# Where the sums of the second MLP leave PSUM, and when GLA's share of the weight sums is made

## The chip, the core and the metric

The kernel runs on one core of a Trainium2 chip. Its engines work side by side, each through its own queue in order: TensorE (matmuls; PE in the profile, its weight loads PEld), VectorE (DVE), ScalarE (ACT), GpSimd (POOL), and SyncE (SP), which here only issues DMAs. A matmul writes its sums into one of eight PSUM banks, and VectorE or ScalarE has to carry them from there to SBUF before the bank can take the next sums. The metric is the device time of one execution in microseconds (us).

## The reference

Two layers over 272 tokens (16 meta tokens and 256 of the sequence) of width 2048. Layer 0 mixes tokens by RWKV-7, layer 1 by gated linear attention (GLA); behind each stands an MLP with squared ReLU:

```python
def sq_relu_mlp(x, w1, w2):
    h = jax.nn.relu(x @ w1)          # 2048 -> 8192
    return (h * h) @ w2              # 8192 -> 2048
...
h = h + mix_out
h = h + sq_relu_mlp(rms_norm(h, norm_mlp[i]), mlp_w1[i], mlp_w2[i])
...
return rms_norm(h, norm_f)[:, N_META:]
```

GLA projects its input to q (4 heads of 256), k (the same), v (4 heads of 512) and a gate (4 heads of 512), runs a chunked recurrence and projects back. Everything is float32; the meta tokens are dropped at the end, so the second MLP works on 256 tokens only.

## The kernel before

**Precision.** A float32 weight tile `raw` (128x1024) is split into two reduced-precision tiles: ScalarE casts it to `hi`, VectorE takes `lo = raw - hi`. The same is done to the moving operand. A float32 product is then three matmuls: hi by hi, hi by lo, lo by hi. So each weight tile costs a DMA, a cast on ScalarE and a subtraction on VectorE. That pair of cast and subtraction is called a split here.

**Order of the work.** RWKV, the first MLP (`mlp`, L268), GLA (`gla`, L1462) and the second MLP (`mlp1`, L371) follow each other. In RWKV partly, and in `mlp1` on all of TensorE, VectorE, ScalarE and SyncE, the order on each engine is that of the program text. In GLA a scheduler orders the queues.

**The second MLP.** The hidden width 8192 is taken in four blocks b of 2048. For each block, a *row* (L408) is a tile of 128 hidden features: two slots of eight wide (512 columns) and eight narrow (256) matmuls; then its two halves are joined (ScalarE copies one, VectorE adds the other), relu and square run on ScalarE, and the result is split into `hi` and `lo` of `HS`. The second matrix product is done in 2x2 blocks by Strassen's scheme in Winograd's form, with seven products for eight. A *unit* (b, g, p), L475, covers 256 hidden features p of block b and one half g of the output columns; the output stands as four quadrants `C[t, f]` in `htok`. A fast unit has four slots, A, B, E and G, with 2, 2, 2 and 1 products of three wide matmuls each. Its seven sums stay in seven PSUM banks `own[1]` to `own[7]` over all p of a phase. An ordinary unit (p beyond `FAST[b]`, block 3 only, where p = 0 to 3 are fast) has two slots with four plain products each, and no gain from the scheme.

The phases run in the order of `PHASES` (L53): (0,1) (0,0) (1,0) (1,1) (2,1) (2,0) (3,0) (3,1). Sums go on over two phases with the same g. So banks are emptied at the ends of phases 0, 2 and 4 (all units fast, `alone` in the code), and of phases 6 and 7 (block 3). In between, rows of this or the next block stand between the units, except before a phase's last unit or two. The four quadrants come out of the seven sums with `t1 = own[1]`, `u2 = own[6] + t1`, `u3 = own[7] + u2`, `u4 = own[5] + u2`:

| quadrant | is increased by, each times a scale per token `rs2` |
|---|---|
| `C[1,0]` | `t1`, `own[2]` |
| `C[1,1]` | `u4`, `own[3]` |
| `C[0,0]` | `u3`, `own[4]` |
| `C[0,1]` | `u3`, `own[5]` |

`into` (L486) is one such increase: one VectorE instruction over 128x512 which reads PSUM or SBUF, multiplies by `rs2` and adds `C`. `t1` and `u2` to `u4` lie in `hres`, the residual stream, which is dead by then; so does `nf`, the final norm's gains, loaded by DMA (L669) at slot 20.

**The stream of slots.** `stream` is the list of all slots. In step i the program emits first what was put down for before slot i, then the split of slot i + 3, then what was put down for behind it, then slot i's matmuls:

```python
for f in before.pop(i, []): f()
while done < min(len(stream), i + AHEAD + 1):   # AHEAD = 3
    split(done); done += 1
for f in behind.pop(i, []): f()
if i < len(stream): stream[i][1](sets.pop(i), i)
```

`later(slot, f, after)` (L391) puts f down for before a slot, or behind its splits where the third argument is true. There are five `raw` buffers and four pairs of `hi` and `lo`. A raw buffer is loaded anew when its split is done; A's and B's only when VectorE has formed, from both, the operand of slot G ("fourth", L641 ff.), a 128x512 subtraction.

**The last phase.** Its p run in the order 0, 4, 1, 5, 2, 3, 6, 7: fast units and ordinary ones in turn. The units p = 6 and 7 (`closes`) first do the products of banks 2 and 3 of all their slots, then those of the other two banks. `gain(t)` multiplies the finished half of `htok` by `nf` (VectorE, 128x1024); `empty` is the last `into` of a bank with the sum of squares on ScalarE; `norm` scales the rows and stores them.

**The weight sums.** The fast units' weights need differences of blocks of `mlp_w2`. These are made ahead: a step fetches three tiles (GpSimd's DMA queue), VectorE forms three differences (L351 to L353, each 128x512), and GpSimd stores them to `diff` in device memory. Of the 56 units, 44 are made in the first MLP and 12 in GLA, with two sets of three tiles in GLA. A unit is fetched in one step, formed in the next, stored in the one after, and so there are 14 steps in GLA. `ticks` (L319) spreads them: each call of `tick` counts up, and the step numbers up to calls x 14 // rows are then made, where `rows` is 27 (L1492). GLA calls `tick` after every key projection, value projection and gate projection, 2 + 4 + 4 times per head. A head's projections run q, k, q, k, four v, four gate; after the second and third gate projection, the next head's forget gates are made (`gate`, L1496, whose matmul L1498 goes to the one bank `pm` and whose VectorE reader is `mn`, L1505).

Of the kernel before, what the change touches and what calls it, by code (L numbers as in the profile page):

```python
# [19 lines left out]
D = 2048  # L20
KT = D // P
# [8 lines left out]
C = 64  # L30
# [30 lines left out]
class Kern:  # L61
# [309 lines left out]
    def mlp1(self, x, acc):  # L371
# [6 lines left out]
        htok = self.t(hp, [P, 2, D], "htok")  # L378
        flat = hres.rearrange("p k t -> p (k t)")
        nf = flat[:, :D]  # L380
        t1, u2, u3, u4 = (flat[:, D + 512 * i : D + 512 * i + 512] for i in range(4))
        ssq = self.t(hp, [P, 2, 4], "ssq")
        sum3 = self.t(hp, [P, 2], "sum3")
        rs2 = self.t(hp, [P, 2], "rs2")
# [6 lines left out]
        def later(slot, f, after=False):  # L391
            (behind if after else before).setdefault(slot, []).append(f)
# [82 lines left out]
        def unit(b, g, p):  # L475
# [20 lines left out]
            if p < FAST[b]:  # L496

                def pe(todo):
                    def run(w, slot):
                        H = hid[p]  # L500
                        for at, i, ws in todo:
                            product(at, (H[:, 0, i], H[:, 1, i]), w, ws, first, final_fast and (alone or at in (1, 5, 6, 7)))
                            if not final_fast:
                                continue
                            if at == 1:
                                later(slot + 1, lambda: nc.scalar.copy(t1, own[1]), True)
                            if at == 2 and alone:
                                later(slot + 1, lambda: into(1, 0, own[2]))
                            if at == 7:
                                later(slot + 1, lambda: (add(u2, own[6], t1), add(u3, own[7], u2)))  # L510
                            if at == 5:
                                later(slot + 2, lambda: (add(u4, own[5], u2), into(0, 1, own[5])))
                                if alone:
                                    later(slot + 3, lambda: into(1, 1, own[3]))
                                later(slot + 3, lambda: into(1, 0, t1))
                                later(slot + 4, lambda: into(1, 1, u4))
                                later(slot + 5, lambda: into(0, 0, u3))
                                later(slot + (5 if end else 6), lambda: into(0, 1, u3))
                            if at == 4 and alone:
                                later(slot + 2, lambda: into(0, 0, own[4]))  # L520
                    return run

                d = self.diff[b, g, p]
                todo = {"A": [(1, 0, one), (2, 2, two)], "B": [(6, 4, two), (7, 5, one)], "E": [(5, 3, two), (3, 6, one)],
                        "G": [(4, 1, one)]}
                srcs = {"A": [(both, w[:, :2])], "B": [(both, d[:, 1:])], "E": [(one, w[:, 2]), (two, d[:, 0])], "G": None}
                return [(srcs[k], pe(todo[k]), k) for k in "ABEG"]
# [14 lines left out]
            def pe(k):  # L542
                def run(w, slot):
                    H = hid[p]
                    if not closes:
                        for at in (2, 3, 4, spare):
                            ordinary(at, H, k, w, last and k == 1)
                        if last and k == 1:
                            for n, at in enumerate((2, 3, 4, spare)):
                                later(slot + 1 + n // 2, lambda at=at: empty(at))  # L550
                            if b == NHB - 1:
                                for n in range(4):
                                    later(slot + 4 + n, lambda n=n: final(n // 2, n % 2))
                        return
                    closing.append((H, k, w))
                    if p == KT // 2 - 2:
                        later(slot + 2, lambda: gain(1 - k))
                    for at in (2, 3):
                        ordinary(at, H, k, w, last and k == 1)
                    if last and k == 1:  # L560
                        empty(2)
                        empty(3)
                        most(1)
                        norm(1)
                        for at in (spare, 4):
                            for n, (X, m, pair) in enumerate(closing):
                                h, ws = places[at][2:]
                                product(at, (X[:, 0, 2 * m + h], X[:, 1, 2 * m + h]), pair, ws, False, n == 3)
                            empty(at)
                            if at == spare:  # L570
                                most(0)
                        norm(0)
                return run
# [3 lines left out]
        def gain(t):  # L577
            tt(htok[:, t, :1024], htok[:, t, :1024], nf[:, :1024], ALU.mult)
# [22 lines left out]
            row(0, f, (0, 4)[f % 2], f if f < 8 else None)  # L601
        for n, (b, g) in enumerate(PHASES):
            second, more = n % 2 == 1, b < NHB - 1
            for p in range(KT // 2) if more or not second else (0, 4, 1, 5, 2, 3, 6, 7):
                if second and more:
                    row(b + 1, p)
                elif not second and b and p < 7:
                    row(b, 9 + p)
                steps = unit(b, g, p)
                stream.extend(steps[:2])  # L610
                if second and more and p == 7:
                    row(b + 1, 8)
                stream.extend(steps[2:])
                if not b and not second and p < 6:
                    row(b, 10 + p)
# [38 lines left out]
        with tc.manual_schedule(engines=engines):  # L654
            load()
            done = 0
            for i in range(len(stream) + 8):
                for f in before.pop(i, []):
                    f()
                while done < min(len(stream), i + AHEAD + 1):  # L660
                    split(done)
                    done += 1
                for f in behind.pop(i, []):
                    f()
                if i < len(stream):
                    stream[i][1](sets.pop(i), i)
                if i == 10:
                    scales()
                if i == 20:  # L669
                    nc.sync.dma_start(nf, ap["nf"].to_broadcast([P, D]))  # L670
        es.close()

# [789 lines left out]
    def gla(self, x, rstd, hres, done):  # L1462
# [26 lines left out]
        pq = self.proj(pair(0), x, SEQ, NMETA)  # L1489
        rs = rstd[:, NMETA:]  # L1490
        left, oT = [[self.t(self.x2p, [P, 2, T], "x", KT) for _ in range(3)] for _ in range(2)], []
        tick = self.ticks(self.differences(slice(EARLY, None), lambda u: left[u % 2], 1), 27)  # L1492
        c0, c1, c2, c3 = (NMETA + C * i for i in range(4))
        gates = {}

# [25 lines left out]
        for hd in range(GH):  # L1521
# [105 lines left out]
            for v in range(4):  # L1627
# [5 lines left out]
                    finish(0, waiting, hr)  # L1633
                gt = self.t(gp, [P, SEQ], "gt", 2)
                tt(self.two(gt), pg, self.two(rs))
                tick(gt[:, :2])
                sg = self.t(gp, [P, SEQ], "sg", 2)
                nc.scalar.activation(sg, gt, AF.Abs)
                nc.scalar.activation(sg, sg, AF.Exp, scale=-1.0)
# [150 lines left out]
```

## Time and profile before

| | |
|---|---|
| median of 3 runs | 2362.39 us (2361.3 to 2363.02) |
| the profiled execution's own time | 2364.6 us |
| its span in the profile | 2362.5 us |
| second MLP within it | first row matmul at 1695.7 us, to the end |
| GLA within it | first forget gate at 1317 us, ends before the second MLP |

All durations below come from the one profiled execution. A line of a queue shows the start in us from the span's start, the duration, the engine, the line, the operation with output and input tiles, and in brackets how long the engine stood idle before it and which instruction's end let it go. In a list of waits stand the total in us, how often, and the longest. Matmuls overlap in their pipeline, so a matmul's bar is longer than its pitch. Tiles are named without numbers: `pu`, `pt`, `pm`, `pry` and `pj` are PSUM banks, which `mlp1` uses as `own[1]`, `own[2]` (`pu`), `own[7]`, `own[6]` (`pt`), `own[5]` (`pm`), `own[3]` (`pry`), `own[4]` and `own[0]` (`pj`).

### The profile page before, as it was taken

How to read it: one execution, taken by the hardware profiler on the slowest of the kernel's cores; microseconds unless marked ns; L12 is line 12 of the kernel's file. 1: busy time of each engine (PE TensorE's matmuls, PEld its weight loads, DVE VectorE, ACT ScalarE, POOL GpSimd, SP SyncE). 2: the span in 40 equal slices, each digit the busy share in tenths (PEclk: the TensorE clock that was granted, in tenths of full speed). 3: DMA queues.
4: the chain of work that ended last, by engine and by line, in shares of the span. 5: the costliest groups of instructions: out<-in, count | busy, mean ns of one | idle time of the engine just before them, and what ended most of it. 6: DMA issues, size and time to landing. Idle time of an engine off the chain costs nothing.

```text
span 2362.5 us, 48857 instructions
## 1 busy us (share of the span) xinstructions
PE 2318.0 (98%) x19183; PEld 2177.1 (92%) x19183; DVE 1821.3 (77%) x2976; ACT 1367.9 (58%) x2152; POOL 222.8 (9%) x541
## 2 busy tenths in 40 slices
PE   9999999999999999999999999999999999999997
PEld 8888888889999999999999999999998898998886
DVE  8868976848667667666666788877779889888877
ACT  6488645556555345345444555556576776776765
POOL 0000000000122222222220023100000000000000
PEclk9999999999999999999999999999999999999999
DMA  6459754535788888888885688755667777877875
GB/s 210 160 195 311 242 164 139 148 98 175 260 300 300 295 308 308 300 303 310 302 286 185 227 272 279 237 170 196 214 214 258 259 267 252 272 257 246 264 251 177
DMA packets 200326, 567.75 MB, mean 240 GB/s; under 512 B 41184, under 2 KB 56800, under 8 KB 199968
## 3 DMA queue, kind: packets, MB, share of 16 engines
q1 hardware_dynamic: 173216, 476.53, 59.6%
q0 software_dynamic: 26880, 88.10, 12.0%
q8 instruction: 151, 2.47, 0.4%
q14 instruction: 79, 0.65, 0.1%
HBM read 504.38 MB, written 58.46 MB: 238 GB/s over the span
## 4 chain that ended last, share of the span: by engine, by line
PE 82%; DVE 11%; ACT 3%; issue 2%; DMA 2%; SPq 0%; DVEq 0%; POOL 0%; ACTq 0%
PE pj L172 16%; PE pj L174 16%; PE pj L173 16%; PE pj L419 9%; PE pj L420 5%; PE pj L205 2%; DVE lo L150 2%; PE pj L206 1%; PE pu L492 1%; PE pu L494 1%; PE pu L493 1%; DVE lo L373 1%; DVE upd L676 1%; DVE sysA L676 1%; PE pt L494 1%
## 5 line engine op out<-in xcount | busy, mean ns | idle before, releaser
L149 ACT CAST hi<-raw 128x1024 fp32r<-128x1024 f32 (+1 forms) x562 | 526.2, 947 | 588.7 <-PE pj L173 508.8
L150 DVE TENSOR_TENSOR lo<-raw,hi 128x1024 fp32r<-128x1024 f32 (+1 forms) x562 | 613.0, 1100 | 247.9 <-ACT hi L149 243.1
L172 PE MATMUL pj<-x,hi 128*128 128x272 f32 (+1 forms) x2560 | 729.2, 285 | 2.0 <-DVE r L676 0.9
L174 PE MATMUL pj<-x,lo 128*128 128x272 f32 (+1 forms) x2560 | 715.3, 279 | 4.4 <-DVE lo L150 4.3
L173 PE MATMUL pj<-x,hi 128*128 128x272 f32 (+1 forms) x2560 | 714.2, 279 | 0.0
L172 PEld LDWEIGHTS pj<-x,hi 128*128 128x128 f32 x2560 | 485.5, 190 | 15.2 <-issue 7.1
L174 PEld LDWEIGHTS pj<-x,lo 128*128 128x128 f32 x2560 | 485.5, 190 | 6.9 <-DVE lo L150 6.6
L173 PEld LDWEIGHTS pj<-x,hi 128*128 128x128 f32 x2560 | 485.6, 190 | 2.5 <-issue 1.4
L373 DVE TENSOR_TENSOR lo<-raw,hi 128x1024 fp32r<-128x1024 f32 x368 | 411.2, 1140 | 72.6 <-ACT hi L641 67.7
L641 ACT CAST hi<-raw 128x1024 fp32r<-128x1024 f32 x368 | 351.5, 979 | 83.1 <-PE pj L419 26.3
L419 PE MATMUL pj<-x,hi 128*128 128x512 f32 x1024 | 341.8, 384 | 1.6 <-ACT hi L641 1.6
L172 PE MATMUL pj<-h,hi 128*128 128x272 f32 x1024 | 285.7, 279 | 0.0
L173 PE MATMUL pj<-h,hi 128*128 128x272 f32 x1024 | 285.7, 279 | 0.0
L174 PE MATMUL pj<-h,lo 128*128 128x272 f32 x1024 | 285.7, 279 | 0.0
L420 PE MATMUL pj<-x,lo 128*128 128x256 f32 x1024 | 280.7, 274 | 2.9 <-DVE lo L373 2.9
L419 PEld LDWEIGHTS pj<-x,hi 128*128 128x128 f32 x1024 | 194.3, 190 | 29.6 <-ACT hi L641 2.8
L420 PEld LDWEIGHTS pj<-x,lo 128*128 128x128 f32 x1024 | 197.2, 193 | 7.0 <-DVE lo L373 5.6
L172 PEld LDWEIGHTS pj<-h,hi 128*128 128x128 f32 x1024 | 193.5, 189 | 0.0
L173 PEld LDWEIGHTS pj<-h,hi 128*128 128x128 f32 x1024 | 193.5, 189 | 0.0
L174 PEld LDWEIGHTS pj<-h,lo 128*128 128x128 f32 x1024 | 193.5, 189 | 0.0
L359 POOL DMA_DIRECT2D diff<-x x168 | 91.6, 545 | 137.6 <-DVE x L353 52.5
L345 POOL DMA_DIRECT2D x<-w_d x168 | 90.1, 542 | 25.3 <-DMA diff<-x 22.8
(352 smaller groups left out, 3415.2 us busy)
## 6 DMA issues: line engine op xcount, KB each, us to landing
raw<-mlp_w_d SPq DMA_DIRECT2D x384, 512.0 KB, 4.9
raw<-gla_in_d SPq DMA_DIRECT2D x98, 512.0 KB, 4.3
x<-w_d POOLq DMA_DIRECT2D x168, 256.0 KB, 5.6
diff<-x POOLq DMA_DIRECT2D x168, 256.0 KB, 6.4
raw<-w_rkv_d SPq DMA_DIRECT2D x80, 512.0 KB, 3.8
raw<-w_d SPq DMA_DIRECT2D x72, 512.0 KB, 4.7
raw<-diff SPq DMA_DIRECT2D x56, 512.0 KB, 5.3
raw<-gla_o_d SPq DMA_DIRECT2D x32, 512.0 KB, 3.3
```

The costliest lines, as they stand in the source:

```text
L149: nc.scalar.copy(hi[:, h], raw[:, h])
L150: nc.vector.tensor_tensor(out=lo[:, h], in0=raw[:, h], in1=hi[:, h].bitcast(F32), op=ALU.subtract)
L172: nc.tensor.matmul(out, hi[:, ws], xh, start=first, stop=False)
L173: nc.tensor.matmul(out, hi[:, ws], xl, start=False, stop=False)
L174: nc.tensor.matmul(out, lo[:, ws], xh, start=False, stop=last)
L205: nc.tensor.matmul(wide, hi[:, ws], xt, start=kt == 0, stop=False)
L345: nc.gpsimd.dma_start(x[:, body], w[:, k])
L359: nc.gpsimd.dma_start(self.diff[b, g, i][:, k], x[:, body])
L373: tt = lambda o, a, b, op: nc.vector.tensor_tensor(out=o, in0=a, in1=b, op=op)
L419: nc.tensor.matmul(wide, hi[:, ws], xt, start=kt == 0, stop=False)
L420: nc.tensor.matmul(narrow, lo[:, ws], xt[:, 0], start=False, stop=kt == KT - 1)
L641: nc.scalar.copy(hi, raw)
```

## The change

Four edits, three of them in `mlp1`:

- At the ends of phases 0, 2 and 4 the sums `own[2]`, `own[3]` and `own[4]` are read by ScalarE, which multiplies them by `rs2` and writes them to `v2`, `v3`, `v4` in `hres`. VectorE adds these to `C` later, from SBUF. Four of the other increases move from the slots right behind the phase's end to later ones: with s the last unit's slot A, the seven operations `into t1`, add `v2`, `into u4`, add `v3`, `into u3`, add `v4`, `into u3` come before slots s+9, s+11, ... s+21. `u4` stays before s+4 and `into(0, 1, own[5])` goes to before s+5.
- As `v2` to `v4` lie where `nf` is loaded, that load moves from slot 20 to the first slot of phase 6.
- The last phase runs its p in the order 0, 4, 1, 2, 3, 5, 6, 7, and `gain` is put down one slot earlier.
- In GLA `tick` is no longer called behind gate projections, and `rows` is 18 in place of 27.

```diff
-        t1, u2, u3, u4 = (flat[:, D + 512 * i : D + 512 * i + 512] for i in range(4))
+        v2, v3, v4, _, t1, u2, u3, u4 = (flat[:, 512 * i : 512 * i + 512] for i in range(8))
...
                             if at == 2 and alone:
-                                later(slot + 1, lambda: into(1, 0, own[2]))
+                                later(slot + 2, lambda: nc.scalar.mul(v2, own[2], rs2[:, 1:2]), True)
...
-                            if at == 5:
+                            if at == 5 and alone:
+                                later(slot + 2, lambda: add(u4, own[5], u2))
+                                later(slot + 3, lambda: into(0, 1, own[5]))
+                                rest = [lambda: into(1, 0, t1), lambda: add(C[1, 0], C[1, 0], v2), lambda: into(1, 1, u4),
+                                        lambda: add(C[1, 1], C[1, 1], v3), lambda: into(0, 0, u3),
+                                        lambda: add(C[0, 0], C[0, 0], v4), lambda: into(0, 1, u3)]
+                                for n, f in enumerate(rest):
+                                    later(slot + 7 + 2 * n, f)
+                            elif at == 5:
                                 later(slot + 2, lambda: (add(u4, own[5], u2), into(0, 1, own[5])))
-                                if alone:
-                                    later(slot + 3, lambda: into(1, 1, own[3]))
...
+                            if at == 3 and alone:
+                                later(slot + 1, lambda: nc.scalar.mul(v3, own[3], rs2[:, 1:2]), True)
                             if at == 4 and alone:
-                                later(slot + 2, lambda: into(0, 0, own[4]))
+                                later(slot + 1, lambda: nc.scalar.mul(v4, own[4], rs2[:, :1]), True)
...
                     if p == KT // 2 - 2:
-                        later(slot + 2, lambda: gain(1 - k))
+                        later(slot + 1, lambda: gain(1 - k))
...
-            for p in range(KT // 2) if more or not second else (0, 4, 1, 5, 2, 3, 6, 7):
+            if n == len(PHASES) - 2:
+                gains_at = len(stream)
+            for p in range(KT // 2) if more or not second else (0, 4, 1, 2, 3, 5, 6, 7):
...
-                if i == 20:
+                if i == gains_at:
                     nc.sync.dma_start(nf, ap["nf"].to_broadcast([P, D]))
...
-        tick = self.ticks(self.differences(slice(EARLY, None), lambda u: left[u % 2], 1), 27)
+        tick = self.ticks(self.differences(slice(EARLY, None), lambda u: left[u % 2], 1), 18)
...
-                tick(gt[:, :2])
```

## The prediction

> **What bounds the kernel now.** I read the busy shares first, then TensorE's waits, then stretches of the second MLP by engine, then both queues instruction by instruction where a stretch has idle TensorE time. The busy shares:
>
> ```profile
> PE 2318.0 (98%) x19183; PEld 2177.1 (92%) x19183; DVE 1821.3 (77%) x2976; ACT 1367.9 (58%) x2152; POOL 222.8 (9%) x541
> ```
>
> TensorE carries the time, and no arithmetic of TensorE is added or taken away. The change can only win back waits. TensorE's waits over the whole run (total us, times, longest):
>
> ```profile
> PE pm L493 <- DVE lo L373: 5.5, 6, 1.7
> ...
> PE pj L420 <- DVE lo L373: 2.9, 6, 0.8
> ...
> PE pj L419 <- ACT hi L641: 1.6, 3, 0.5
> PE pm L1498 <- DVE mn L1505: 1.4, 2, 0.7
> ```
>
> The first three are in the second MLP: TensorE stands at a `lo` that VectorE has not written. The fourth is GLA's gate. Where in the second MLP, by stretches (length, then PE, PEld, DVE, ACT, POOL busy, clock, DMA share, GB/s):
>
> ```profile
> 1810.00:1840.00 30.00, 26.56 (x132) 21.50 (x131) 28.18 (x38) 18.27 (x24) 0.00 (x0) 1.00 0.71 232
> 1840.00:1970.00 130.00, 130.00 (x708) 116.86 (x707) 112.50 (x141) 94.40 (x129) 0.00 (x0) 1.00 0.80 266
> 1970.00:2000.00 30.00, 26.56 (x132) 21.50 (x131) 28.14 (x38) 18.93 (x25) 0.00 (x0) 1.00 0.68 234
> ...
> 2132.00:2162.00 30.00, 26.56 (x123) 21.31 (x122) 28.00 (x37) 17.88 (x24) 0.00 (x0) 0.95 0.70 234
> ...
> 2350.00:2362.00 12.00, 0.00 (x0) 0.00 (x0) 4.53 (x9) 5.26 (x14) 0.00 (x0) 0.64 0.53 175
> ```
>
> TensorE is idle 3.44 us in each of three stretches, and not at all in the 130 us between. The three are the ends of phases 0, 2 and 4, where seven PSUM sums are emptied; VectorE is 94% busy there, ScalarE 61%. TensorE's queue at the first (start, duration):
>
> ```profile
> 1810.67 0.38 PE L492 MATMUL pu<-hi,HS 128*128 128x512 f32 x1
> ...
> 1820.56 0.38 PE L419 MATMUL pj<-x,hi 128*128 128x512 f32 x1
> ...
> 1834.99 0.38 PE L420 MATMUL pj<-x,lo 128*128 128x256 f32 x1 [0.78 <-DVE lo L373]
> 1835.20 0.38 PE L419 MATMUL pj<-x,hi 128*128 128x512 f32 x1
> 1835.42 0.27 PE L420 MATMUL pj<-x,lo 128*128 128x256 f32 x1
> 1835.53 0.38 PE L419 MATMUL pj<-x,hi 128*128 128x512 f32 x1
> ```
>
> Undisturbed, a wide matmul starts 0.22 after the last (0.216 over many) and a narrow one 0.11. By the code there stand 80 wide and 16 narrow ones from 1810.67 up to 1834.99 (three fast units of 21, a row of 16 and 16, one more wide): 80 x 0.216 + 16 x 0.11 = 19.0 of 24.3 us. So a phase end loses 5.3 us, more than the idle figure, because bars of 0.38 that start 0.22 apart hide short gaps. Three of them: 16 us, the ceiling of what this part can give. VectorE's queue over the same place:
>
> ```profile
> 1819.20 0.75 DVE L487 SCALAR_TENSOR_TENSOR htok<-pu,rs,htok 128x512 f32<-128x512 f32 x1
> 1819.86 1.22 DVE L373 TENSOR_TENSOR lo<-raw,hi 128x1024 fp32r<-128x1024 f32 x1
> ...
> 1824.66 0.68 DVE L373 TENSOR_TENSOR hres<-pm,hres 128x512 f32<-128x512 f32 x1
> 1825.26 0.74 DVE L487 SCALAR_TENSOR_TENSOR htok<-pm,rs,htok 128x512 f32<-128x512 f32 x1
> 1825.92 1.21 DVE L373 TENSOR_TENSOR lo<-raw,hi 128x1024 fp32r<-128x1024 f32 x1
> 1827.05 0.68 DVE L373 TENSOR_TENSOR raw<-raw,raw 128x512 f32<-128x512 f32 x1
> 1827.65 0.74 DVE L487 SCALAR_TENSOR_TENSOR htok<-pry,rs,htok 128x512 f32<-128x512 f32 x1
> ...
> 1828.97 0.74 DVE L487 SCALAR_TENSOR_TENSOR htok<-pj,rs,htok 128x512 f32<-128x512 f32 x1
> 1829.63 1.21 DVE L373 TENSOR_TENSOR lo<-raw,hi 128x1024 fp32r<-128x1024 f32 x1
> 1830.77 0.74 DVE L487 SCALAR_TENSOR_TENSOR htok<-hres,rs,htok 128x512 f32<-128x512 f32 x1
> 1831.43 0.41 DVE L373 TENSOR_TENSOR cj<-pj,cj 128x256 f32<-128x256 f32 x1
> 1831.76 0.68 DVE L373 TENSOR_TENSOR lo<-raw,hi 128x512 fp32r<-128x512 f32 x1
> ...
> 1833.71 1.22 DVE L373 TENSOR_TENSOR lo<-raw,hi 128x1024 fp32r<-128x1024 f32 x1 [0.61 <-ACT hi L641]
> ```
>
> From start to start: a split 1.14, a 512-wide add 0.60, an emptying (L487) 0.66, a row's join 0.33. Call the last unit's slot of A s; the row after it is s+4 and s+5, the next unit A to G s+6 to s+9, the row after that s+10 and s+11.
>
> **Phase ends: the edit.** Before s+10's split the old queue has seven emptyings (`own[2]`, `own[5]`, `own[3]`, `t1`, `own[4]`, `u4`, `u3`); the new one keeps only `own[5]`. Three sums go to ScalarE as scaled copies; the rest, four emptyings and three adds, goes one per second slot to s+9 ... s+21. ScalarE's rows:
>
> ```profile
> 1819.05 0.58 ACT L506 COPY hres<-pu 128x512 f32<-128x512 f32 x1
> ...
> 1822.08 1.05 ACT L641 CAST hi<-raw 128x1024 fp32r<-128x1024 f32 x1 [1.50 <-DMA raw<-w_d]
> ...
> 1832.65 3.87 ACT L641 CAST hi<-raw 128x1024 fp32r<-128x1024 f32 x4
> ```
>
> A scaled copy of a bank is not in this trace; the plain one takes 0.58, and I take 0.6 (0.58 to 0.75, the price of VectorE's). The Trainium skill, "ScalarE: Activation LUTs", section "Rules for kernel authors", says to multiply on VectorE and not on ScalarE, which speaks against this edit. By that rule the three multiplies stay on VectorE, and the sum would be 3 x 0.66 = 2.0 us worse at a phase end; the stretch rows above, 28.18 us against 18.27, say that VectorE is the engine without room here.
>
> The new queue of VectorE, by these prices: split s+4 1819.20 to 1820.34 (no emptying ahead); adds `u2`, `u3` to 1821.54; split s+5 to 1822.7; split s+6 waits for its `hi` (raw tile there at 1822.08, plus 1.05) and runs 1823.13 to 1824.27; `u4` to 1824.87; split s+7 to 1826.0; the fourth operand to 1826.6; `own[5]` to 1827.26; split s+8 to 1828.4; join to 1828.73. From the join's end, relu, square and `hi` follow on ScalarE, then s+10's split: 1833.71 - 1831.76 = 1.95 after it before, so 1830.68 to 1831.82 now. The three copies (1.8 us) stand between ScalarE's casts and end before 1825.4; none of them makes a `lo` late by this walk. TensorE: the row s+4 starts at 1820.56, unit s+6 at 1825.8, row s+10 at 1830.35, where it again waits, but only to 1831.8; s+8's `lo` at 1828.4 is just in time. The narrow matmul of 1834.99 so comes at about 1831.9: **3.1 us won**.
>
> **What is late next.** Between phase ends VectorE is busy 112.50 of 130 us; of a group of six slots (21 fast matmuls and a row, 9.8 us) 1.3 us are free. Into two such groups now come 4 x 0.66 + 3 x 0.60 = 4.4 us where 2.6 are free, so up to 1.8 us return as new stalls in front of the rows. Some of it the splits' lead of three slots absorbs: I take 1.2, between 0 and 1.8. Net per phase end 3.1 - 1.2 = 1.9 (1.3 to 3.1), for three 5.7 us (3.9 to 9.3).
>
> **Clock.** In the third stretch the granted clock is 0.95 on the mean, in its two twins 1.00: 0.05 x 30 = 1.5 us lost to half clock after the same stalls. I expect it gone, -1.5, but it may come back elsewhere (0 to -1.5). The Trainium skill, "TensorE: Matmul & The Clock Gate", section "What's actually happening", says that a free-running window of about 3.4 us of too little activity halves the clock: by it, which phase end is hit is chance, and spread stalls should hit none. One of three alike agrees.
>
> **GLA.** The differences step leaves the gate loop; it is three 512-wide subtractions, 1.8 us of VectorE, just ahead of the gate's `mn`. Both waits of L1498 (1.4 us, 0.7 each) lie right behind such a step and should go: -1.4. The same steps now run in key and value projections, closer together:
>
> ```profile
> x<-w_d POOLq DMA_DIRECT2D x168, 256.0 KB, 5.6
> diff<-x POOLq DMA_DIRECT2D x168, 256.0 KB, 6.4
> ```
>
> Cost there between 0 and the rival below; I take 0.
>
> **Last phase.** TensorE's first matmul of p=6, VectorE's first last-emptying, and its last:
>
> ```profile
> 2338.84 0.38 PE L492 MATMUL pu<-hi,HS 128*128 128x512 f32 x1
> ```
>
> ```profile
> 2348.00 0.74 DVE L487 SCALAR_TENSOR_TENSOR htok<-pu,rs,htok 128x512 f32<-128x512 f32 x1
> ...
> 2353.87 0.74 DVE L487 SCALAR_TENSOR_TENSOR htok<-pj,rs,htok 128x512 f32<-128x512 f32 x1
> ```
>
> TensorE is done before 2350; VectorE's queue sets the end: its first last-emptying starts 9.16 us behind p=6. In the new order p=5, two ordinary slots (24 matmuls, 5.2 us, but two splits, 2.3 us, of VectorE), stands between the fast sums' emptying and p=6: 2.9 us of room. The bound from below: the last split needs the buffers of p=5's second half, free at p=6's start; then a cast 0.95, a split 1.14, `u3` twice 1.32, two gains of 1.14 (1024 wide, as a split), about 5.9 with hand-overs: 3.1 us earlier than 9.16. If VectorE enters p=3 without lead, its work from there is 15.2 us against 7.15 of TensorE's up to p=6: 8.05, 1.1 earlier. The last chain (5.87 us from 2348.00 to 2353.87, then the norm and the stores) moves with it. I take -2.5. Against it, three fast units now follow each other, 3 x 1.14 + 2 x 0.60 = 4.62 us of VectorE for 21 x 0.216 = 4.53 of TensorE each, and three tiles of 0.52 MB, 347 GB/s, where 266 GB/s cost a share of 0.80: a ceiling near 333. I take +0.3 (0 to 1.5). The 1.05 MB load of `nf`, moved into a busier stage, costs 3.2 us of DMA at that ceiling; five raw tiles and three split slots lie ahead of TensorE, so 0, or up to 3.2 if that cover is gone.
>
> **Sum.** -5.7 - 1.5 - 1.4 - 2.5 + 0.3 = -10.8 us. The profiled execution took 2364.6 (span 2362.5), so 2353.8; the median of the runs, 2362.39, stands 2.2 lower: **2351.6 us**.
>
> **Rivals.**
> Everything hides (0.17): the spread work costs nothing and the row s+10 does not wait; 0.8 us per phase end remain. 3 x 4.5 + 1.5 + 1.4 + 3.1 = 19.5: 2343. For it: TensorE had no idle time in 130 us; against it: the 86%.
> Given back later (0.16): the 4.4 us per phase end return in full and s+8 is late too, so phase ends win nothing: 2362.4 - 1.4 - 2.5 = 2358.5.
> The edit isn't what decides (0.10): a raw tile was already late at 1822.08 (1.50 us). If weights limit the phase end, only GLA, the clock and half of the tail move: 2362.4 - 4.1 = 2358.3.
> Slower (0.07): differences steps in neighbouring projections. One projection with its surroundings takes 6.2 us:
>
> ```profile
> L1464 DVE TENSOR_TENSOR gt<-pj,acc x16: 406/421/425, 1368.9 to 1611.9; 128x256 f32<-128x256 f32 x16
> ```
>
> (three heads of 12 and three more projections in 243 us). Two sets of tiles give two projections, 12.4 us, to form (1.8), store (6.4) and fetch again (5.6): 13.8. By the counters of the code seven steps follow a step in the projection just before. If VectorE stands at its next form, the splits queued behind stand too. TensorE has the lead of the hi/lo buffers; from 2.0 us per step on (7 x 2.0 = 14.0) it eats the other 9.4 us and 4.6 more. At 2.3 us: 2362.4 - 9.4 + 16 = 2369.
>
> **How the numbers follow.** The forecast has 0.50. Its own range is 2347 to 2357. The range to 2343 takes in the first rival, that to 2360 the two about 2358; left out are the slower one and the far ends. About 0.2%, 4.7 us, is what a measurement can tell: faster is below 2357.7. That is the forecast, the first rival, and half of the two in the middle: 0.80. Same 0.13, slower 0.07.
>
> **What would show it.** Right: idle TensorE at each phase end falls from 3.44 to below 2.5 us, the wait of L493 at the eighth slot is nearly gone, short waits of L420 stand some 10 and 20 us later, no wait of L1498, clock 1.00 throughout, the first last-emptying 6 to 7 us behind p=6. Wrong: L493 still waits over 1 us; TensorE waits in GLA's value projections while VectorE waits for a fetch; ScalarE's copies delay a `hi`.

## The result and the profile after

| | before | after |
|---|---|---|
| median (13 runs each) | 2363.02 us (2361.3 to 2371.94) | 2371.47 us (2367.46 to 2375.66) |
| profiled execution, span | 2364.6, 2362.5 us | 2372.69, 2370.8 us |
| GLA: first gate matmul to the first row of the second MLP | 378.6 us | 393.0 us |
| second MLP: from there to the end | 666.8 us | 660.9 us |

The changed kernel is slower: ratio 1.0031, 95% interval 1.0021 to 1.0041. The forecast was 10.8 us less. The two regions went opposite ways: the MLP won 5.9 us, GLA lost 14.4. The busy shares do not show it:

```profile
PE 2322.7 (98%) x19183; PEld 2180.6 (92%) x19183; DVE 1818.4 (77%) x2976; ACT 1372.1 (58%) x2161; POOL 219.5 (9%) x541
```

TensorE has the same 19183 matmuls, yet 4.7 us more busy time: a sign that some of them ran slower, and GLA shows where, below. TensorE's waits over the run:

```profile
PE pj L420 <- DVE lo L373: 5.4, 7, 0.8
...
PE pt L1585 <- DVE Am L1474: 4.1, 2, 3.2
...
PE pu L1598 <- DVE Vl L1474: 2.0, 2, 1.3
PE pt L1585 <- DVE KX L1564: 1.9, 1, 1.9
PE pt L1620 <- DVE vs L1474: 1.5, 2, 1.0
...
PE pt L1620 <- DVE Am L1474: 1.1, 1, 1.1
...
PE pm L493 <- DVE lo L373: 0.8, 4, 0.3
```

L493's wait in the MLP fell from 5.5 us to 0.8, and the gate's wait on `mn` (1.4) is gone; both were wanted. New are five groups in GLA, 10.6 us together, all on what VectorE writes in key and value projections. The MLP's phase ends and the stretch between the first two, in the columns of before (14.2 us later in the span):

```profile
1824.00:1854.00 30.00, 28.82 (x147) 24.18 (x146) 27.80 (x37) 21.89 (x32) 0.00 (x0) 1.00 0.74 249
1854.00:1984.00 130.00, 129.19 (x704) 115.65 (x703) 114.38 (x145) 93.43 (x125) 0.00 (x0) 1.00 0.81 266
1984.00:2014.00 30.00, 28.90 (x148) 24.50 (x147) 27.45 (x36) 21.67 (x32) 0.00 (x0) 1.00 0.78 254
...
2146.00:2176.00 30.00, 28.53 (x143) 23.83 (x142) 27.71 (x40) 21.89 (x32) 0.00 (x0) 1.00 0.75 248
```

Idle TensorE at a phase end fell from 3.44 us to 1.18, 1.10 and 1.47; the clock is 1.00 in all three; and 0.81 us of idling stands where none was, in the 130 us behind.

**The loss in GLA, at its largest place.** Head 1's first value projection: VectorE's queue, then GpSimd's, then TensorE's.

```profile
1418.49 0.43 DVE L1474 TENSOR_TENSOR vs<-pj,acc 128x272 f32<-128x272 f32 x1
1422.47 0.69 DVE L351 TENSOR_TENSOR x<-x,x 128x513 f32<-128x513 f32 x1 [3.55 <-POOL x L350]
...
1424.82 0.41 DVE L1474 TENSOR_TENSOR Am<-pt,gc 80x256 f32<-80x256 f32 x1
```

```profile
1421.13 0.54 POOL L345 DMA_DIRECT2D x<-w_d  x1 [3.71 <-DMA diff<-x]
...
1422.26 0.18 POOL L350 COPY x<-vs 128x2 f32<-128x2 f32 x1
```

```profile
1425.29 1.12 PE L1585 MATMUL pt<-Q,KX 128*128 128x64 f32 x4 [3.20 <-DVE Am L1474]
...
1426.76 0.43 PE L172 MATMUL pj<-x,hi 128*128 128x272 f32 x1
1426.98 0.43 PE L173 MATMUL pj<-x,hi 128*128 128x272 f32 x1
```

Read from below. L1585 is the matmul of `weights()` in the code, which makes three groups of sums from `Q` and `KX`, while there are two `pt` banks; so the third group needs the bank that VectorE empties when it makes the first `Am`. TensorE stands 3.20 us for this `Am`, which VectorE writes at 1424.82, though it was done with `vs` at 1418.9. Ahead of `Am` stands the differences step's first subtraction, and VectorE waits 3.55 us to begin it, for a copy of two columns by GpSimd. That copy stands behind the issue of the next fetch, which waited 3.71 us until an earlier store had left the tile that it fills. So the wait of a spare transfer became a wait of TensorE. After it TensorE's matmuls start 0.22 apart, where the 272-wide ones had started 0.115 apart (1421.23, 1421.35, 1421.46): half clock. By windows of 4 us:

```profile
1420.00:1424.00 4.00, 2.09 (x18) 1.89 (x17) 1.52 (x2) 0.00 (x0) 1.59 (x4) 1.00 0.93 343
1424.00:1428.00 4.00, 2.71 (x12) 2.71 (x12) 3.02 (x8) 0.76 (x2) 2.96 (x6) 0.51 0.71 192
1428.00:1432.00 4.00, 4.00 (x26) 3.63 (x26) 1.90 (x4) 1.63 (x4) 0.54 (x1) 0.63 0.83 297
```

The granted clock is 0.51 and 0.63 there, and 0.61 once more at 1520 to 1524, behind waits of 0.73 and 1.05 us. (1 - clock) times length over GLA is 5.1 us. Half clock is busy time to the profile, which is why PE's busy total rose while it did no more work.

### The profile page after: what moved, and what is told of

It is laid out like the page before. It is cut to its first block, busy times and chain, and to the rows that moved or that the text cites. A ratio compares the mean times of both kernels' runs of the same rounds, so it can differ in the third digit from the quotient of the medians.

```text
span 2370.8 us, 48875 instructions
## 1 busy us (share of the span) xinstructions
PE 2322.7 (98%) x19183; PEld 2180.6 (92%) x19183; DVE 1818.4 (77%) x2976; ACT 1372.1 (58%) x2161; POOL 219.5 (9%) x541
## 4 chain that ended last, share of the span: by engine, by line
PE 73%; DVE 15%; ACT 5%; DMA 4%; issue 3%; POOL 0%; SPq 0%; DVEq 0%; ACTq 0%; POOLq 0%
PE pj L172 15%; PE pj L174 14%; PE pj L173 14%; PE pj L419 8%; PE pj L420 4%; DVE lo L150 3%; PE pj L205 2%; DVE lo L373 2%; ACT hi L149 1%; PE pj L206 1%; DVE upd L686 1%; DVE sysA L686 1%; ACT hi L651 1%; PE pu L492 1%; PE pu L494 1%
## 5 line engine op out<-in xcount | busy, mean ns | idle before, releaser
L419 PE MATMUL pj<-x,hi 128*128 128x512 f32 x1024 | 340.6, 383 | 0.4 <-ACT hi L651 0.3
L419 PEld LDWEIGHTS pj<-x,hi 128*128 128x128 f32 x1024 | 193.5, 189 | 28.8 <-ACT hi L651 2.6
L420 PEld LDWEIGHTS pj<-x,lo 128*128 128x128 f32 x1024 | 196.4, 192 | 10.6 <-DVE lo L373 9.5
```

What stands on the lines that cost most here:

```text
L419: nc.tensor.matmul(wide, hi[:, ws], xt, start=kt == 0, stop=False)
L420: nc.tensor.matmul(narrow, lo[:, ws], xt[:, 0], start=False, stop=kt == KT - 1)
```

## The experiments

**Theories.** Queue: a step's form, waiting for its tiles, holds everything queued behind it on VectorE. Work (called load in the expectations): the 1.8 us of subtractions in busier projections suffice. DMA: the steps' transfers delay GLA's weights. For the MLP: what the spread operations cost depends on how many there are, or on where they stand.

GLA's length can be accounted for: 376.2 us, plus TensorE's waits in it, plus the clock's loss, gives each kernel's GLA to within 1.8 us (376.2 is fitted to the first row; the others test it). "Clock" is (1 - clock) times length; it also charges half clock that falls into a wait, where it costs nothing: 0.6 us of it in the changed kernel, 1.0 in e2 and 1.7 in e6, which is why e6's sum comes out too large.

| kernel | waits | clock | sum | GLA measured | MLP |
|---|---|---|---|---|---|
| e3, no forms | 0.6 | 0 | 376.8 | 376.8 | 660.3 |
| before | 1.4 | 0 | 377.6 | 378.6 | 666.8 |
| e1, MLP edits alone | 1.7 | 0 | 377.9 | 379.5 | 663.2 |
| e5, no stores | 3.4 | 1.7 | 381.3 | 382.1 | 661.8 |
| e4, forms on a tile of their own | 4.8 | 1.7 | 382.7 | 382.9 | 662.1 |
| e11, step behind its projection's work | 4.2 | 0 | 380.4 | 382.2 | 662.7 |
| e12, the same, gates too, 27 ticks | 4.6 | 1.7 | 382.5 | 383.5 | 655.9 |
| e2, GLA edit alone | 9.3 | 3.4 | 388.9 | 389.8 | 668.8 |
| after | 10.6 | 5.1 | 391.9 | 393.0 | 660.9 |
| e6, query projections too | 12.9 | 12.0 | 401.1 | 399.7 | 662.1 |

The last column has a use of its own. After, e1, e3, e4, e5, e6 and e11 run the same second MLP (e5 reads other blocks), and it took 660.3 to 663.2 us; before and e2 share the old one, at 666.8 and 668.8. So one profile of the MLP against another shows nothing below some 3 us.

**The two halves alone: e1_mlp_only and e2_gla_only.** The first is the changed kernel with this undone, the second the kernel before with only this done:

```diff
-        tick = self.ticks(self.differences(slice(EARLY, None), lambda u: left[u % 2], 1), 27)
+        tick = self.ticks(self.differences(slice(EARLY, None), lambda u: left[u % 2], 1), 18)
...
-                tick(gt[:, :2])
```

> The changed kernel with its GLA edit undone (27 rows, a tick behind gate projections again). From GLA's first forget gate to the second MLP's first row takes 378.6 us before and 393.0 us after, from there to the end of the span 666.8 and 660.9. If the whole loss is GLA's: GLA back at 378 to 380 us, the second MLP at 661, time about 2357 us. Rival, the second MLP's edits cost something that the profile of after hides (for example through GLA's DMAs): time 2363 or more.

> The kernel before with the GLA edit alone. If GLA's loss is its own: GLA 391 to 395 us, second MLP 666 to 668, time about 2377 us. If it needs the other edits: 2363 us.

The MLP's edits alone: 2358.7 us against 2363.63, ratio 0.9977 (0.9967 to 0.9986). GLA's edit alone: 2375.21, ratio 1.005 (1.0035 to 1.0065). They add up, within the intervals: -0.23% and +0.50% against the +0.31% of both. The whole loss is GLA's.

**What in GLA's steps costs: e3_gla_noform, e4_gla_scratch, e5_gla_nostore.** All three are the changed kernel with something left out, one run each. e3 leaves out the three subtractions (fetches and stores stay). e4 makes three subtractions of the same size on a tile that no DMA touches; like e3, it stores the fetched blocks as they are. e5 forms the differences and doesn't store them; the MLP then reads other units' differences.

```diff
 e3
+            if not forms:
+                return
             tt(out=x22[:, wide], in0=x22[:, wide], in1=x12[:, wide], op=ALU.subtract)
...
 e4
+            if scratch is not None:
+                s = scratch
+                nc.vector.tensor_copy(s[:, 511:513], mark)
+                for n in (wide, body, body):
+                    tt(out=s[:, n], in0=s[:, n], in1=s[:, n], op=ALU.subtract)
+                return
...
 e5
-            for x, k in ((t1, 0), (t3, 1), (t2, 2)):
+            for x, k in ((t1, 0), (t3, 1), (t2, 2)) if stores else ():
```

> The changed kernel; in GLA's steps the three VectorE subtractions are left out, so for the last 12 units the blocks themselves and not their differences are stored. All fetches and stores stay where they are. Three theories of GLA's 14 us. Queue: VectorE stands at a step's first subtraction until the tile chain of store and fetch is through, and all behind it waits: GLA 378 to 382 us. Load: 1.8 us of VectorE work more in projections that were nearly full: GLA 378 to 382 us too. DMA: the denser fetches and stores hold GLA's weight tiles back: GLA stays near 393 us.

> The changed kernel; in GLA's steps the three VectorE subtractions are made at the same places with the same sizes, but on a tile of their own, which no DMA touches; for the last 12 units the fetched blocks are stored unchanged. Queue: the waiting is gone and only the work stays, GLA 379 to 383 us. Load: the work is what costs, GLA 389 to 394 us. DMA: GLA near 393 us.

> The changed kernel; GLA's steps fetch and subtract, but store nothing, and the second MLP reads another block's differences for those 12 units. A tile set is then free for the next fetch as soon as VectorE has done with it. GLA took 393.0 us after, 382.9 with the subtractions on a tile of their own, 376.8 without them. Queue: what VectorE waits for is the store's landing before the next fetch can be issued, so the waits for GpSimd's copy fall from 14.4 us to under 4, GLA 378 to 384 us. If the fetch alone is too slow for the next projection: waits stay over 8 us, GLA 386 to 392 us.

2354.43, 2363.41 and 2359.83 us. With the same transfers and no form, GLA is 1.8 us shorter than before, so the DMA theory falls; ScalarE's wait for GLA's weights is 20.4 us there and 18.0 before, and nothing came of it. The subtractions by themselves cost 6 us (382.9 - 376.8), the waits for tiles some 10 more (393.0 - 382.9). Without the stores ahead of the fetches (e5, 382.1) the latter are gone: VectorE's waits for GpSimd's copy were 14.4 us in the changed kernel, and are 4.5 in e5 and 4.1 before. So both queue and work, queue the larger, each by one run.

**Fewer steps in a row: e6_gla_spaced.** Ticks behind the query projections as well, and 24 rows, so that steps lie further apart.

```diff
-        tick = self.ticks(self.differences(slice(EARLY, None), lambda u: left[u % 2], 1), 18)
+        tick = self.ticks(self.differences(slice(EARLY, None), lambda u: left[u % 2], 1), 24)
...
+                tick(qf[:, :2])
                 tt(q[:, : 3 * C], qf[:, : 3 * C], eb[:, c0:c3])
```

> The changed kernel with a tick behind query projections too and 24 rows: the same 14 steps end at the same projection, but only 4 in place of 7 follow a step in the projection just before, and never three in a row. Queue: GLA's loss goes with steps in a row, GLA 381 to 387 us. Load: key and first value projections are as full as after, and the query projections are fuller, GLA 390 to 395 us.

2380.46 us in one run: worse, against the queue theory as I had put it, by the number of steps in a row. TensorE's longest waits in its GLA:

```profile
1425.91 4.24 PE L1586 MATMUL pt<-Q,KX 128*80 128x192 f32 x18 [5.26 <-DVE KX L1565]
...
1512.43 1.12 PE L1586 MATMUL pt<-Q,KX 128*128 128x64 f32 x4 [3.67 <-DVE Am L1474]
```

Both are L1586, the matmuls of `weights()`: TensorE reads a head's `KX` as soon as VectorE has written it, and then needs the bank that VectorE's `Am` empties. A step in the last key projection or the first value projection of a head stands just there. By this one run, the distance of steps counts for less than whether one falls on this place.

**The place in the queue: e11_gla_behind, e12_both_places.** e11 is the changed kernel with `tick` at the end of a projection's own work (behind `KX`, behind `Vl`). e12 is e9 (below, GLA as before) with the same, and in the gate loop behind the next head's gate, 27 rows.

```diff
-                tick(ks[:, :2])
...
                 tt(run[:, 4 * C : 5 * C], ks[:, c2:c3], dec[:, c2:c3])
+                tick(ks[:, :2])
...
-                tick(vs[:, :2])
...
                     tt(Vl[:, :, vc], p3, Vh[:, :, vc].bitcast(F32), ALU.subtract)
+                tick(vs[:, :2])
```

> The changed kernel with only the place of GLA's steps moved: the same fourteen steps in the same projections, but each stands at the end of its projection's own work on VectorE (behind KX in a key projection, behind Am and Vl in a value projection) instead of ahead of it. Order theory (what costs are the form's wait and 1.8 us standing ahead of KX, Am and Vl that TensorE needs next): the waits on Am, Vl and KX, 10 us in all, are nearly gone, GLA 381 to 385 us, median 2360 to 2364. Landing theory (a step waits for the store ahead of it to land wherever it stands, and holds what is queued behind it): the waits move to vs, ks and the next projections, GLA 389 to 394, median 2368 to 2372.

> e9_mlp_holes, and GLA's steps as in the kernel before (27 ticks, the gate loop among them), but each step at the end of its projection's own work on VectorE, in the gate loop behind the next head's gate. If the place in the queue decides and not which projection carries a step, the waits of the gate on mn (1.4 us before) go with no new ones: GLA 376.5 to 378 us, second MLP 655 to 655.5, median 2348.5 to 2351. If it is the gate loop that is at fault wherever the step stands there, the wait on mn stays: GLA 378.5 to 380, median 2351 to 2353.

e11: 2362.56 us, ratio to before 0.9993 (0.9984 to 1.0002), some 9 us less than the changed kernel by an edit of place alone. TensorE waits 4.2 us instead of 10.6, and the clock holds. VectorE still stands 11.0 us for GpSimd's copies (14.4 in the changed kernel), but TensorE waits less for what is queued behind. The rows of its waits in GLA:

```profile
PE pt L1619 <- DVE vs L1474: 1.6, 2, 1.1
PE pt L1585 <- DVE Am L1474: 1.4, 2, 1.0
PE pm L1508 <- DVE mn L1515: 0.7, 1, 0.7
PE pu L1598 <- DVE Vl L1474: 0.5, 1, 0.5
```

e12 missed: 2355.64 us, ratio 0.9965 (0.9951 to 0.9978), 4 us slower than e9 (on another chip; the profiles put it in GLA, 383.5 us against 379.4). The gate's wait is gone, but TensorE waits 1.91 us for `Am` at 1418.75. Its VectorE queue at head 1's `weights()`, and then that of the kernel before:

```profile
1414.87 0.69 DVE L351 TENSOR_TENSOR x<-x,x 128x513 f32<-128x513 f32 x1
1415.59 0.69 DVE L352 TENSOR_TENSOR x<-x,x 128x512 f32<-128x512 f32 x1
...
1417.34 0.68 DVE L353 TENSOR_TENSOR x<-x,x 128x512 f32<-128x512 f32 x1
1417.94 0.43 DVE L1474 TENSOR_TENSOR vs<-pj,acc 128x272 f32<-128x272 f32 x1
1418.29 0.41 DVE L1474 TENSOR_TENSOR Am<-pt,gc 80x256 f32<-80x256 f32 x1
```

```profile
1410.53 0.70 DVE L351 TENSOR_TENSOR x<-x,x 128x513 f32<-128x513 f32 x1 [0.20 <-POOL x L350]
...
1413.09 0.68 DVE L353 TENSOR_TENSOR x<-x,x 128x512 f32<-128x512 f32 x1
...
1415.68 0.43 DVE L1464 TENSOR_TENSOR vs<-pj,acc 128x272 f32<-128x272 f32 x1
1416.11 0.42 DVE L1464 TENSOR_TENSOR Am<-pt,gc 80x256 f32<-80x256 f32 x1
```

Before, the same step in the same projection is threaded between `KX`'s parts, which have time, and done 2 us before `vs`. "Behind its own work" means, in the last key projection, "ahead of `weights()`". What fits e6, e11 and e12 together is neither the projection nor ahead or behind, but the distance to the next thing that TensorE needs at once from VectorE, a result or an emptied bank; a run that changes this distance alone was not made.

**The load of `nf`: e7_mlp_nf.** e1 with the load at the first ordinary unit of phase 6 (p=4).

```diff
-            if n == len(PHASES) - 2:
-                gains_at = len(stream)
...
+                if n == len(PHASES) - 2 and p == FAST[b]:
+                    gains_at = len(stream)
                 steps = unit(b, g, p)
```

> The changed kernel without the GLA edit, and with the load of nf at the first ordinary unit of phase 6, where DMA is light. After, TensorE lost 1.7 us near 2262 us (2.8 near 2250 in the run without the GLA edit), a weight tile standing behind that load. If the load is the cause: that stall is gone, the second MLP 660 to 661 us, time about 2356.5 us. Rival, a tile would have been late there anyway: no change from 2358.7 us.

The load was issued at 2247.65 in the changed kernel. The two transfers of the weight tile issued right behind it landed 8.2 and 8.5 us after their issue; the same two in e7, without the load ahead of them, 5.9 and 6.1. ScalarE's cast of the late tile in the changed kernel, the same cast in e1, and TensorE's wait in the changed kernel:

```profile
2257.13 1.04 ACT L651 CAST hi<-raw 128x1024 fp32r<-128x1024 f32 x1 [3.73 <-PE pj L420]
```

```profile
2244.80 1.05 ACT L651 CAST hi<-raw 128x1024 fp32r<-128x1024 f32 x1 [3.40 <-DMA raw<-diff]
```

```profile
2262.92 0.38 PE L420 MATMUL pj<-x,lo 128*128 128x256 f32 x1 [0.78 <-DVE lo L373]
```

In e1 the cast's wait is put down to the tile; in the changed kernel to a matmul that ended just after the tile had landed. TensorE's start gaps lose 1.7 us at that place in the changed kernel, 2.8 in e1 and 0.4 in e7, so the stall there is the load's. The whole time does not show it: e7 measured 2357.59 us, ratio 0.9974 (0.9964 to 0.9984), its MLP took 660.8 us, within the 660.3 to 663.2 of the kernels with the load at the old place, and the medians (2358.7 and 2357.59, on two chips) are too near to tell them apart.

**The spread operations: e8_mlp_nf_stride, e9_mlp_holes, e10_mlp_full.** e8 is e7 with them before every third slot. e9 puts the same seven into the places where VectorE waits for a cast. In e10 ScalarE also copies the other four sums, and VectorE's eleven operations follow one or two a group.

```diff
-                                    later(slot + 7 + 2 * n, f)
 e8
+                                    later(slot + 7 + 3 * n, f)
 e9
+                                    later(slot + (5, 17, 17, 29, 29, 41, 41)[n], f)
 e10
+                                rest = [lambda: add(u2, u2, t1), lambda: add(u3, u3, u2), lambda: add(u4, v5, u2),
+                                        lambda: into(0, 1, v5), lambda: into(1, 0, t1),
...
+                                    later(slot + (5, 11, 17, 17, 23, 29, 29, 35, 41, 41, 47)[n], f)
```

> As the run with nf at the ordinary units, and with the seven spread operations one per third slot (s+9 to s+27) in place of every second. If VectorE's room between phase ends decides (1.3 us per six slots, now filled with 1.3 and not 2.0): the two later stalls of L420 at each phase end (0.2 and 1.0 us) go, the second MLP 656.5 to 658 us, time about 2353 us. Rival, the stalls come from the raw tiles or ScalarE: they stay, 2356.5 us.

> GLA as before, nf's load at the first ordinary unit of phase 6; the seven spread operations of a phase end stand at s+7 (one), s+19, s+31 and s+43 (two each), ahead of the row's split for which VectorE waits 1.27 us on ScalarE's cast, instead of every second slot. Place theory (an operation costs where it stands right ahead of a row's join, and nothing where VectorE stands idle for a cast): the stalls of 0.96 to 0.98 us at s+22 go, second MLP 657 to 658.5 us, median 2354 to 2355.5. Amount theory (VectorE has no room for these operations wherever they stand): a stall of the same size comes at another row, second MLP 660 to 661, median 2357.

> As e9_mlp_holes, and ScalarE also copies the other four PSUM sums (t1, own[5], own[6], own[7]: seven copies at a phase end, one to two a slot), so that VectorE empties no PSUM there at all; its eleven operations follow one or two a group of six slots. VectorE theory (the rest of the phase end's loss is VectorE's queue ahead of the row s+10): the stall there, 0.34 and 1.04 us at the first end, goes as well, second MLP 653 to 656 us, median 2349.5 to 2353. ScalarE theory (seven copies of 0.58 us in five slots, ahead of the casts that the splits wait for, make the splits late): second MLP 660 or more, median 2357 or more.

e8: 2357.09 us, ratio 0.9968 (0.9958 to 0.9978), no better than e7; 2353 was not reached. Wider spacing left the second stall of a phase end where it was. VectorE in e8, ahead of TensorE's wait of 0.78 us at 1852.12, and then ScalarE's relu:

```profile
1847.95 0.68 DVE L373 TENSOR_TENSOR htok<-htok,hres 128x512 f32<-128x512 f32 x1
1848.56 0.41 DVE L373 TENSOR_TENSOR cj<-pj,cj 128x256 f32<-128x256 f32 x1
1848.89 0.68 DVE L373 TENSOR_TENSOR lo<-raw,hi 128x512 fp32r<-128x512 f32 x1
1850.84 2.36 DVE L373 TENSOR_TENSOR lo<-raw,hi 128x1024 fp32r<-128x1024 f32 x2 [1.27 <-ACT hi L651]
```

```profile
1849.01 0.42 ACT L441 ACTIVATE cj<-cj 128x256 f32<-128x256 f32 x1 [1.45 <-DVE cj L373]
```

The add stands right ahead of the row's join (`cj`), for which ScalarE's relu (L441) waits. Relu, square and the cast on ScalarE wait for the join, the split for the cast: the add costs its 0.6 us in this chain, and two lines below it VectorE is idle for 1.27 us. e9 puts two operations into just that gap:

```profile
1847.86 0.68 DVE L373 TENSOR_TENSOR htok<-htok,hres 128x512 f32<-128x512 f32 x1
1848.46 0.75 DVE L487 SCALAR_TENSOR_TENSOR htok<-hres,rs,htok 128x512 f32<-128x512 f32 x1
1849.13 2.35 DVE L373 TENSOR_TENSOR lo<-raw,hi 128x1024 fp32r<-128x1024 f32 x2
```

```profile
1840.00:1970.00 130.00, 130.00 (x711) 116.88 (x711) 115.15 (x144) 93.79 (x127) 0.00 (x0) 1.00 0.80 267
```

TensorE idles nowhere in the 130 us, though VectorE is busier (115.15 us; 114.38 in the changed kernel). e9 measured 2351.65 us, ratio 0.9948 (0.9935 to 0.996), the MLP 655.3 us: better than my own expectation (2354 to 2355.5), since the shorter stalls at other rows went too. The operations and their count are those of e8, whose MLP took 660.3 us, and the 5 us between the two are more than the same MLP varies: place decides. e10: 2350.72, ratio 0.9945 (0.9932 to 0.9957), which can't be told from e9. One stall of 1.04 us is left at s+10 in both. In e10 VectorE's split there waits for ScalarE, which has worked on copies and casts for 8 us up to it without a listed break:

```profile
1828.29 2.36 DVE L373 TENSOR_TENSOR lo<-raw,hi 128x1024 fp32r<-128x1024 f32 x2 [0.48 <-ACT hi L653]
```

So e9, with GLA left as it was, beats both kernels, by 0.5% and, going by the ratios to before, 0.8%.

## Why the prediction was wrong, step by step

**GLA: "Cost there between 0 and the rival below; I take 0." is the step that failed**, and with it "The change can only win back waits." Measured: GLA took 14.4 us more. TensorE's waits there rose from 1.4 to 10.6 us, and half clock adds up to 5.1. The rival "Slower" had most of the mechanism and nearly the time: 2369 forecast, 2371.47 measured, though part of the nearness is luck, since it priced GLA at 16 us and the MLP's gain at 9.4, and both were smaller (14.4 and 5.9). It had rows for it (13.8 us for a turn of the tiles against 12.4), and I gave it 0.07; the one thing that the text sets against it is TensorE's lead of hi and lo buffers, without a number. That lead is one of weights. What TensorE came to wait for are not splits but `KX`, `vs` and `Vl`, which it reads soon after VectorE writes them, and the banks that `Am` empties. That was to be read in the code and in the kernel before, where `Am` follows `vs` at once. Nor did the rival price the clock, about a third of the loss. The -1.4 for the gate's wait was right by itself: it went (in e12 too), and e3, with the transfers and no forms, is 1.8 us below before.

**Phase ends: right.** From the first fast matmul of the last unit (1810.67, now 1824.83) the walk put the narrow matmul of row s+10 at 1831.9 on the old scale, and 1846.26 - 14.16 is 1832.1:

```profile
1824.83 0.38 PE L492 MATMUL pu<-hi,HS 128*128 128x512 f32 x1
...
1846.26 0.38 PE L420 MATMUL pj<-x,lo 128*128 128x256 f32 x1 [0.78 <-DVE lo L373]
...
1867.20 0.38 PE L420 MATMUL pj<-x,lo 128*128 128x256 f32 x1 [0.78 <-DVE lo L373]
```

Won: 2.9 for a forecast 3.1. Given back: 1.4 by 1870, for a forecast 1.2, mostly in the stall 21 us later, as the text had it. Its reason was half right: VectorE had room, the operations stood in the wrong places (e9). (Of the three rows of waits that the prediction puts down to `lo`, the third, L419's, names ScalarE's `hi`; no term hangs on it.) A scaled copy took 0.69 us against 0.6 taken (bounds 0.58 to 0.75).

```profile
1834.63 0.69 ACT L508 ACTIVATE hres<-pu,rs 128x512 f32<-128x512 f32 x1
```

The rule of the Trainium skill quoted there, "ScalarE: Activation LUTs", section "Rules for kernel authors", to multiply on VectorE, did not hold here: the multiply took 0.69 us on ScalarE, the multiply and add together 0.74 to 0.75 on VectorE, and ScalarE had the time (busy 21.89 of the 30 us). VectorE's work hardly shrinks by it, as an add of 0.60 us stays for each emptying of 0.66; what is won is that it comes later. How much of the 2.9 us is due to the three copies, and how much to the later place of the other increases, no run separates.

**Clock: right in the MLP.** Counted by the starts of the matmuls, the three phase ends and what is given back behind them lose 11.8 us, half clock included, where before they lost 17.8: 6.0 won, for 5.7 and 1.5 forecast. The prediction used the clock for what the change takes away and not for what it adds. In GLA, the clock records of these traces show windows: in the changed kernel half clock lasts from 1424.1 to 1430.9 and from 1519.7 to 1523.1, two windows of 3.41 us and one, and the two starts are 28 windows apart. Whether a window is followed by half clock goes by how long TensorE idles within it: over all GLA traces, of the windows entered at full clock, all seven with over 1.7 us of idling were followed by it, two of the three with 1.6 to 1.7, and none with less. The wait of 1.88 us that ends at 1418.34 in the changed kernel fell into two windows, 0.83 and 1.05 us, and nothing came of it; so whether a wait of some 2 us costs clock goes by where it falls. e2's second MLP, the old code, has half clock behind the first two phase ends (from 1843.5 and from 2007.3) and not behind the third; before had it behind the third alone (from 2158.8). The Trainium skill, "TensorE: Matmul & The Clock Gate", section "What's actually happening", has a free-running window of about 3.4 us, with which this agrees, and names an idle window as what halves the clock; here half of one was enough.

**Last phase: right way, too large.** p=6 now starts at 2348.45 and the first last-emptying 7.83 us behind it, for "6 to 7" and bounds down from 8.05; before it was 9.16.

```profile
2348.45 0.38 PE L492 MATMUL pu<-hi,HS 128*128 128x512 f32 x1
```

```profile
2356.28 0.75 DVE L487 SCALAR_TENSOR_TENSOR htok<-pu,rs,htok 128x512 f32<-128x512 f32 x1
```

1.3 us won for 2.5. (The lower bound, 9.16 less 5.9, is 3.3 us earlier and not 3.1.) VectorE enters p=3 without lead, which is the second bound of the text, since a weight tile came late. ScalarE's cast and VectorE's split behind it:

```profile
2339.07 2.69 ACT L651 CAST hi<-raw 128x1024 fp32r<-128x1024 f32 x3 [2.45 <-DMA raw<-diff]
```

```profile
2340.16 2.96 DVE L373 TENSOR_TENSOR lo<-raw,hi 128x1024 fp32r<-128x1024 f32 x3 [1.66 <-ACT hi L651]
```

From there to the emptying at 2356.28 VectorE has no break. That the three fast units in a row made the tile late fits the 347 GB/s of the text, but no run with another order tests it.

**`nf`:** taken at 0, the price of a lost cover at up to 3.2; it cost 1.3 at its place (1.7 against e7's 0.4). By these terms the MLP's 9.4 became 5.9: phase ends and clock 1.2 short, tail 0.9 (2.2 with the fast units' 0.3, 1.3 measured), `nf` 1.3.

What stays open: the up to 1.8 us by which the GLA sum falls short of its rows; short gaps that the waits do not list would fit, but this is not shown. A third set of tiles for GLA's steps was not tried.

## What to carry to other kernels

Work that is squeezed beside a tuned stage costs by the distance to the next thing that the bounding engine needs at once, a result or an emptied bank, so look in the queue for where the filling engine already waits for another, and put the work there; counting free microseconds of the stage misses it both ways. If a moved step also waits for a transfer, put a price on that wait at the worst place it can fall, and add the clock that a stall of 2 or 3 us can cost after it is over. A rival that has rows for it and is set aside by "there is a lead" needs that lead shown at every place where the step can stand.

## What the runs showed of the hardware

The clock's loss beside the waits that went with it was 5.1 us to 10.6 in the changed kernel and 12.0 to 12.9 in e6, less what fell into the waits themselves (0.6 and 1.7). At the wait of 3.20 us half clock began at 1424.1, while TensorE still stood, and went on for 5.6 us behind the wait, to 1430.9; it hides in the busy time. A GpSimd copy of two columns, 0.18 us by itself, held VectorE for 3.55 us because of what stood ahead of it in GpSimd's queue.
